# Layer 0 attention: the gates are read in place as strided columns instead of being copied for each unit

## The chip, the cores and the metric

The kernel runs on one core of a Trainium2 chip. The metric is the device time of one execution in microseconds (us); several executions are given with their median. TensorE does matrix products, VectorE and ScalarE work elementwise on SBUF and PSUM, GpSimd works elementwise on SBUF alone, and SyncE issues the DMAs. In the profile TensorE is PE (its weight loads are PEld), VectorE is DVE, ScalarE is ACT, GpSimd is POOL and SyncE is SP.

## The reference

A decoder of two layers on 1024 tokens of width 1024. Layer 0 mixes by attention with three branches, each over the same query head, and adds the three results weighted by a sigmoid gate that depends on the token, the head and the branch:

```python
gates = jax.nn.sigmoid(gate_logit + gate_b).reshape(B, S, N_MIX_HEADS, 3)
...
p_cmp = masked_softmax(s, cmp_end[None, :] <= t[:, None])      # 63 compressed blocks
o_cmp = einsum(p_cmp, vc)
o_slc = einsum(masked_softmax(s, m_sel), vg)                   # causal, 1024 keys
o_win = einsum(masked_softmax(s, m_win), vw)                   # window of 512 keys
return g[..., 0:1] * o_cmp + g[..., 1:2] * o_slc + g[..., 2:3] * o_win
```

There are 12 heads in 2 groups; 4 more heads attend to 256 memory tokens without a gate. No compressed block is visible to the first 31 tokens, so `o_cmp` is zero in those rows: the kernel reaches this by setting the compressed branch's gate to zero there (the row mask `self.rv`, one where the token's row is at least 31 and zero before). A convolutional feed-forward part follows each layer's attention; layer 1 has attention without gates.

## The kernel before, in words

Tokens lie on the 128 partitions in 8 tiles. `layer0_proj` (L706) projects them; the gate logits of tile t go to `self.gates[:, t, :]` (a tile of 128 x 8 x 36 numbers, 36 being 12 heads by 3 branches, branch last), by L755, and one sigmoid on ScalarE over all of it (L756) ends that. `self.gates` stays in SBUF.

`layer0_attn` then runs 24 gated units, one for each head h and each half c of the tokens (512 queries, four tiles of 128), and 8 memory units between them. The generator `units0` describes a unit: the selected branch (tile `ps`), the window branch (`pw`) and the compressed branch (`pc`), the last scored jointly with the window. The function `attention` (L446) is one loop of steps that interleaves a unit's stages, several units deep: a unit's `load` and its scores (PE, L300) begin about 9 steps ahead of its own value steps. In a step, DVE and ACT and POOL do:

- `lift` (L330, DVE): score plus mask from PSUM into `ps`, `pw` or `pc`, and the row minimum of the negated scores into `stat`.
- L343 and L346 (ACT): the exponentials, with their sums.
- L354 and L355 (DVE): 1 / max(sum, 1e-30) in `stat`, on 128 x 4 or 128 x 8 numbers.
- L366 (POOL): the probabilities times that reciprocal times the gate, a tile of 128 queries at a time, each with two numbers per partition as scalars (`r[:, ii:ii+1]` and `gate[:, ii:ii+1]`); for the compressed branch L360 (POOL) multiplies the four reciprocals by the four gates, and L362 (POOL) applies them to `pc`.
- L399 (PE): transposes the probabilities into PSUM (`psb`); L406 (ACT) and L409 (DVE) split them into a high and a low part in `pt`; L422 (PE) multiplies them by the values.

Besides, POOL adds the halves of finished outputs (L481, `wr`) and does one step of the rotary embedding (L623, `rt`).

`load` in `units0` also makes the unit's own copy of the gates: a tile `gt` (128 x 3 x 4, two buffers) is filled by a copy on DVE (L836), and for the first half (c = 0) the row mask is multiplied into one column (L838, DVE). Since `gt` has two buffers, the copy of one unit overwrites the `gt` of the unit two before it, and the last reader of that is the unit's L360 on POOL. The framework's scheduler sets the order of instructions on each engine and puts semaphore waits where tiles are reused; each engine runs its instructions in that order.

Of the kernel before, what the change touches and what calls it, by code (L numbers as in the profile page):

```python
# [8 lines left out]
F32 = mybir.dt.float32  # L9
# [3 lines left out]
ALU = mybir.AluOpType  # L13
# [4 lines left out]
P = 128  # L18
# [20 lines left out]
def f32(ap):  # L39
    return ap.bitcast(F32)  # L40


class Trunk:
# [674 lines left out]
    def layer0_proj(self, cpool):  # L718
        nc, a, tc = self.nc, self.a, self.tc
        w = a["a_w_in"][0]  # L720
        self.mem = []
        self.qd0 = self.dp.tile([2, 2, NH * 32, S], F32, name="qd0")
        self.kd0 = self.dp.tile([2, 2, 4 * 32, S], F32, name="kd0")
        self.vd0 = self.dp.tile([S, 4, 2 * HD], F32, name="vd0")
        self.qm0 = self.dp.tile([2, NMH * HD, S], F32, name="qm0")
        self.gates = self.cp.tile([P, NT, NH * 3], F32, name="gates")
        self.kc = self.cp.tile([P, NG, 64], F32R, name="kc")
        self.vc = self.cp.tile([P, NG, 2, HD], F32R, name="vc")
        with tc.tile_pool(name="l0p", bufs=1) as pool:
            h = [self.hpair() for _ in range(2)]  # L730
            xs = []

            def load_x(t):
                xs.append(self.sb(pool, [P, D], F32, "xl", 2))
                nc.sync.dma_start(xs[t], a["x"][0, t * P:(t + 1) * P, :])

            def norm(t):
                self.norm_t(pool, xs[t], gb, h[t // 4][0], h[t // 4][1], (t % 4) * P)
            load_x(0)
            gb = self.gain(pool, a["attn_norm"][0:1, :], 2)  # L740
            wv = self.load_block(w, [(1152, 128), (1408, 164)])
            gbias = pool.tile([P, NH * 3], F32, name="gbias")
            nc.sync.dma_start(gbias, a["a_gate_b"].to_broadcast([P, NH * 3]))
            norm(0)
            for t in range(NT):
                if t + 1 < NT:
                    load_x(t + 1)
                    norm(t + 1)
                ps = self.psb()[:, 0:292]
                hh, hl = h[t // 4]  # L750
                o = (t % 4) * P
                for kt in range(KT):
                    self.mm3(ps, (hh[:, kt, o:o + P], hl[:, kt, o:o + P]), wv(kt, 0, 292), kt == 0, kt == KT - 1)
                self.store_v(pool, ps[:, 0:256], self.vd0[t * P:(t + 1) * P], 4)
                nc.vector.tensor_tensor(self.gates[:, t, :], ps[:, 256:292], gbias, ALU.add)  # L755
            nc.scalar.activation(self.gates, self.gates, AF.Sigmoid)  # L756
            self.masks(pool, cpool)
            ct = pool.tile([P, 2, 32], F32, name="ct")
            nc.sync.dma_start(ct, a["rope_cmp"])
            comp = [self.compress(pool, h, w, kind, ct) for kind in range(2)]  # L760
            mems = [self.mem_kv(pool, l) for l in range(2)]
            keys = self.rope_proj(cpool, h, w, [(1024, 128), (1280, 128)], self.kd0, 0, None)
            first = self.rope_proj(cpool, h, w, [(0, 256)], self.qd0, 0, QSC)
            order = "k cc kkk m kkk dd kkkk m kkk c kkk m d q m c q m c q m d q m d q n c q n d q n c q n d qq n qq n q n qqqqqq"
            gens = {"k": keys, "q": first, "c": comp[0], "d": comp[1], "m": mems[0], "n": mems[1]}
            for name in order.replace(" ", ""):
                next(gens[name], None)
            for g in (comp[0], comp[1], mems[0], mems[1], first):
                for _ in g:
                    pass  # L770
        return h
# [23 lines left out]
    def units0(self, ap):  # L795
        nc = self.nc
        t_s, t_w, t_c = [("ps0", 1280, 1), ("ps1", 3328, 1)], [("pw0", 1280, 1), ("pw1", 2560, 1)], ("pc", 256, 2)
        for g in range(NG):
            kk, vv = {}, {}
            vc = self.vc[:, g].rearrange("n s d -> n (s d)")  # L800
            for h in range(g * 6, g * 6 + 6):
                for c in range(2):
                    sp_c = {ii: (0, 64, self.m_cmp[:, c * 4 + ii, :]) for ii in range(4)}
                    sp_w = {}
                    for ii in range(4):
                        i = c * 4 + ii
                        k0 = max(0, i - 4) * P
                        sp_w[ii] = (k0, (i + 1) * P, self.m_win if i >= 4 else self.m_cau[:, S - (i + 1) * P:])
                    brs = [{"spans": self.causal(c, self.m_cau), "kb": P, "p": t_s[c], "on": "pool"},
                           {"spans": sp_w, "kb": P, "p": t_w[c], "on": "pool"},  # L810
                           {"spans": sp_c, "kb": 64, "p": t_c, "on": "pool"}]

                    brs[1]["joint"] = brs[2]

                    def load(g=g, h=h, c=c, kk=kk, vv=vv, vc=vc, brs=brs):
                        if not kk:
                            for b in range(2):

                                kk[b] = self.sb(ap, [P, NT, 192] if b else [P, NT, P], F32R, f"kk{b}", 1)
                                for i in range(2):  # L820
                                    for half in range(2):
                                        p0, r0 = i * HD + half * 32, (b * NG + g) * 32
                                        nc.sync.dma_start(f32(kk[b][p0:p0 + 32, :, 0:P]), self.kd0[i, half, r0:r0 + 32, :].rearrange("r (t n) -> r t n", n=P))
                                if b:
                                    nc.vector.tensor_copy(kk[b][:, :, P:], f32(self.kc[:, g, :]).rearrange("p (o n) -> p o n", o=1).to_broadcast([P, NT, 64]))
                                vt = self.sb(ap, [P, NT, P], F32R, "vv", 2)
                                nc.sync.dma_start(f32(vt), self.vd0[:, b * NG + g, :].rearrange("(t p) d -> p t d", p=P))
                                vv[b] = vt
                        q = [self.sb(ap, [P, CH], F32R, f"qq{i}", self.n_q if i else 2) for i in range(2)]
                        for i in range(2):  # L830
                            for half in range(2):
                                for x in range(2):
                                    p0 = (i ^ x) * HD + half * 32
                                    nc.sync.dma_start(f32(q[x][p0:p0 + 32, :]), self.qd0[i, half, h * 32:(h + 1) * 32, c * CH:(c + 1) * CH])
                        gt = self.sb(ap, [P, 3, 4], F32, "gt", 2)
                        nc.vector.tensor_copy(gt, self.gates[:, c * 4:(c + 1) * 4, h * 3:(h + 1) * 3].rearrange("p t b -> p b t"))  # L836
                        if c == 0:
                            nc.vector.tensor_tensor(gt[:, 0, 0:1], gt[:, 0, 0:1], self.rv, ALU.mult)  # L838
                        for b in range(2):
                            k = kk[b] if b else kk[b].rearrange("p t n -> p (t n)")  # L840
                            brs[b].update(q=q, k=(k, k), v=lambda j, v=vv[b]: v[:, j, :], gate=gt[:, 1 + b, :])
                        brs[2].update(v=lambda j: vc, gate=gt[:, 0, :])
                    yield {"branches": brs, "load": load, "needs": [("q", h // 4)] if h >= 4 else [], "at": (h, c)}


# [722 lines left out]
```

## Time and profile before

| what | value |
|---|---|
| median of 3 runs | 2611.74 us |
| the runs | 2602.53, 2613.72, 2611.74 us |
| profiled execution, first to last instruction (span) | 2602.7 us |
| profiled execution, time of its own around the span | none listed apart from the runs |
| PE, DVE, ACT, POOL busy over the span | 95%, 73%, 52%, 29% |
| layer 0 attention in the trace | about 165 to 645 us |
| POOL instructions on gates: L366, L360 | 192, 24 |
| DVE instructions on `gt`: L836, L838 | 24, 12 |

In rows of the timeline the columns are start in us, duration in us, engine, line, operation, what is written and read, count, and in brackets the engine's idle time just before and what ended it. Rows of waits give the waiting engine and what it waited for, then the total in us, the number of waits, the longest. Rows of groups give the busy time and the mean duration in ns, then the idle time ahead of the group.

### The profile page before, as it was taken

The page shows a single profiled execution, that of the slowest core. Times are in us where ns is not written, and L with a number is a line of the kernel's source. Part 1 is how long each engine was busy: PE and PEld are TensorE (multiplying, and loading weights), DVE is VectorE, ACT ScalarE, POOL GpSimd, SP SyncE. Part 2 cuts the span into 40 slices and gives each one's busy share as a digit, 9 for nine tenths or more (in the row PEclk, how much of TensorE's full clock was granted, in tenths as well). Part 3 has the DMA queues.
Part 4 walks back from the last instruction along what each step waited for, and adds up shares of the span by engine and source line. Part 5 has one row for each costly group of instructions (what it writes and reads, how often), then busy time and mean ns, then how long its engine had stood idle before and what let it go on. Part 6 is the DMA issues. An engine that isn't in the chain of part 4 may idle for free.

```text
span 2602.7 us, 35727 instructions
## 1 busy us (share of the span) xinstructions
PE 2466.1 (95%) x12306; PEld 2058.2 (79%) x12306; DVE 1887.8 (73%) x3207; ACT 1342.2 (52%) x2553; POOL 751.8 (29%) x616
## 2 busy tenths in 40 slices
PE   7898988988999999998999999999999999998998
PEld 7787777766778888886888988887777888886886
DVE  5757787888377878877665467878476778787765
ACT  5437777877145454443454356767244444443443
POOL 0105344444134554543000000000233455444000
PEclk9999999999999999999999999999999999999999
DMA  8473224333422333347334466666622233237523
GB/s 250 145 206 111 62 82 114 104 105 125 163 74 89 113 101 98 105 169 268 108 128 137 153 186 189 199 180 176 211 101 76 95 105 114 98 100 278 172 97 114
DMA packets 302701, 357.69 MB, mean 137 GB/s; under 512 B 37960, under 2 KB 183224, under 8 KB 302520
## 3 DMA queue, kind: packets, MB, share of 16 engines
q1 hardware_dynamic: 302520, 355.41, 42.9%
q8 instruction: 97, 1.59, 0.3%
q14 instruction: 84, 0.69, 0.1%
HBM read 245.55 MB, written 109.78 MB: 137 GB/s over the span
## 4 chain that ended last, share of the span: by engine, by line
PE 71%; DVE 10%; ACT 6%; DMA 5%; POOL 4%; issue 3%; SPq 0%; POOLq 0%; ACTq 0%; DVEq 0%
PE psa L157 12%; PE psa L158 12%; PE psa L159 12%; PE psb L157 9%; PE psb L159 9%; PE psb L158 8%; PE psa L300 3%; PE psb L399 3%; PE psb L422 3%; DVE pt L409 2%; ACT pt L406 1%; POOL gs L1360 1%; DVE ps L330 1%; POOL pw L366 1%; DVE wl L82 1%
## 5 line engine op out<-in xcount | busy, mean ns | idle before, releaser
L81 ACT ACTIVATE wh<-wr 128x512 fp32r<-128x512 f32 (+2 forms) x254 | 193.0, 763 | 357.6 <-PE psb L159 146.2
L82 DVE TENSOR_TENSOR wl<-wr,wh 128x512 fp32r<-128x512 f32 (+2 forms) x254 | 241.1, 953 | 166.8 <-ACT wh L81 166.1
L1345 DVE SCALAR_TENSOR_TENSOR v<-u,cw,v 128x1023 f32<-128x1023 f32 (+1 forms) x176 | 283.1, 1608 | 68.7 <-ACT v L1343 68.5
L409 DVE TENSOR_TENSOR pt<-psb,pt 128x512 fp32r<-128x512 f32 (+2 forms) x380 | 246.6, 658 | 62.1 <-ACT pt L406 59.0
L1343 ACT ACTIVATE v<-u,cw 128x1024 f32<-128x1024 f32 x88 | 109.6, 1246 | 309.9 <-DVE u L1332 283.2
L406 ACT ACTIVATE pt<-psb 128x512 fp32r<-128x512 f32 (+2 forms) x380 | 213.4, 571 | 88.7 <-PE psb L399 83.5
L422 PE MATMUL psb<-pt,vv 128*128 128x512 f32 (+2 forms) x864 | 225.8, 356 | 17.3 <-DVE pt L409 13.2
L157 PE MATMUL psa<-hT,wh 128*128 128x512 f32 x560 | 219.2, 392 | 5.3 <-DVE u L1306 5.3
L159 PE MATMUL psa<-hT,wl 128*128 128x512 f32 x560 | 218.7, 391 | 0.8 <-DVE wl L82 0.8
L158 PE MATMUL psa<-hT,wh 128*128 128x512 f32 x560 | 218.6, 390 | 0.0
L300 PE MATMUL psa<-kk,qq 128*128 128x512 f32 (+4 forms) x792 | 186.1, 350 | 20.1 <-DVE stat L330 12.3
L343 ACT ACTIVATE ps<-ps,stat 128x128 f32<-128x128 f32 (+1 forms) x192 | 147.8, 771 | 56.8 <-DVE stat L330 56.3
L422 PEld LDWEIGHTS psb<-pt,vv 128*128 128x128 f32 x864 | 141.4, 191 | 42.2 <-DVE pt L409 21.7
L121 POOL TENSOR_TENSOR rs<-ss,consts 128x1 f32<-128x1 f32 x44 | 25.8, 588 | 511.2 <-DVE ss L119 372.5
L481 POOL TENSOR_TENSOR wr<-wr 128x512 f32<-128x512 f32 x32 | 41.4, 1300 | 427.4 <-DMA kd<-st 244.5
L399 PE MATMUL psb<-consts,ps 128*128 128x128 f32 x928 | 149.2, 279 | 14.5 <-DVE pt L409 7.5
L157 PE MATMUL psb<-wh 128*128 128x512 f32 x352 | 139.8, 397 | 20.7 <-ACT wh L81 20.6
L157 PE MATMUL psb<-hT,wh 128*128 128x512 f32 x384 | 156.6, 408 | 1.0 <-DVE pt L409 0.9
L1247 POOL TENSOR_TENSOR ws<-wr 128x512 f32<-128x512 f32 x44 | 67.7, 1539 | 295.3 <-DMA wr<-in_w_up_dram 276.2
L159 PE MATMUL psb<-hT,wl 128*128 128x512 f32 x384 | 151.2, 394 | 0.0
L158 PE MATMUL psb<-hT,wh 128*128 128x512 f32 x384 | 150.8, 393 | 0.0
L300 PEld LDWEIGHTS psa<-kk,qq 128*128 128x128 f32 x792 | 121.6, 194 | 36.1 <-DVE stat L330 13.8
(287 smaller groups left out, 6831.0 us busy)
## 6 DMA issues: line engine op xcount, KB each, us to landing
wr<-in_w_up_dram SPq DMA_DIRECT2D x88, 512.0 KB
wr<-gd SPq DMA_DIRECT2D x154, 256.0 KB
gd<-v SPq DMA_DIRECT2D x88, 256.0 KB
gd<-gs SPq DMA_DIRECT2D x66, 256.0 KB
o<-ob SPq DMA_DIRECT2D x128, 128.0 KB
wr<-o SPq DMA_DIRECT2D x32, 512.0 KB
hT<-in_w_down_dram SPq DMA_DIRECT2D x64, 256.0 KB
qd<-st SPq DMA_DIRECT2D x56, 256.0 KB
```

The costliest lines, as they stand in the source:

```text
L81: nc.scalar.activation(hi, src, AF.Copy)
L82: nc.vector.tensor_tensor(lo, src, f32(hi), ALU.subtract)
L157: mm(out, lh, rh, start=first, stop=False, skip_group_check=more)
L158: mm(out, lh, rl, start=False, stop=False, skip_group_check=more)
L159: mm(out, ll, rh, start=False, stop=last, skip_group_check=more)
L300: nc.tensor.matmul(out, w, rhs, start=b not in banks[:i], stop=b not in banks[i + 1:])
L343: nc.scalar.activation(p, p, AF.Exp, bias=st[:, 0, ii:ii + 1], scale=-1.0, accum_out=st[:, 1, ii:ii + 1])
L399: nc.tensor.transpose(tp[0:kb, x:x + P], br["pt"][ii][:, o:o + kb], self.ident)
L406: nc.scalar.activation(st["hi"], st["src"], AF.Copy)
L409: self.nc.vector.tensor_tensor(st["lo"], st["src"], f32(st["hi"]), ALU.subtract)
L422: self.nc.tensor.matmul(out, v, t, start=st["begin"] and i == 0, stop=st["end"] and i == len(mms) - 1)
L1345: nc.vector.scalar_tensor_tensor(v[:, d:], u[:, :S - d], cw[:, tap, i:i + 1], v[:, d:], ALU.mult, ALU.add)
```

## The change

After the sigmoid one instruction on DVE multiplies the row mask into the compressed branch's gate of all 12 heads in the first token tile, in place (12 numbers in a partition, 3 apart). The tile `gt` and its copy and mask for each unit go; a unit's gates are now slices of `self.gates` of four numbers in a partition, 36 numbers (144 bytes) apart.

```diff
             nc.scalar.activation(self.gates, self.gates, AF.Sigmoid)
+            g0 = self.gates.rearrange("p t (h b) -> p t h b", b=3)[:, 0, :, 0]
+            nc.vector.tensor_scalar(g0, g0, self.rv, None, ALU.mult)
...
-                        gt = self.sb(ap, [P, 3, 4], F32, "gt", 2)
-                        nc.vector.tensor_copy(gt, self.gates[:, c * 4:(c + 1) * 4, h * 3:(h + 1) * 3].rearrange("p t b -> p b t"))
-                        if c == 0:
-                            nc.vector.tensor_tensor(gt[:, 0, 0:1], gt[:, 0, 0:1], self.rv, ALU.mult)
+                        gt = [self.gates[:, c * 4:(c + 1) * 4, h * 3 + b] for b in range(3)]
                         for b in range(2):
                             k = kk[b] if b else kk[b].rearrange("p t n -> p (t n)")
-                            brs[b].update(q=q, k=(k, k), v=lambda j, v=vv[b]: v[:, j, :], gate=gt[:, 1 + b, :])
-                        brs[2].update(v=lambda j: vc, gate=gt[:, 0, :])
+                            brs[b].update(q=q, k=(k, k), v=lambda j, v=vv[b]: v[:, j, :], gate=gt[1 + b])
+                        brs[2].update(v=lambda j: vc, gate=gt[0])
```

The lines behind it move: L836 and L838 are gone, and the new instruction is L758 of the changed kernel. Lines up to L756, all of `attention` and its helpers among them, keep their numbers.

On DVE, where the scores of one unit are lifted and the copy for the next unit stands among them (the names are tiles with the program's numbers, what waits is in brackets), the kernel before has:

```order
L330 ISA ps_417_2563,stat_2562<-psa_2553,caub 128x128 [waits PE_49]
L330 ISA stat_2562 128x1
L330 ISA ps_417_2563,stat_2562<-psa_2553,caub 128x256
L330 ISA stat_2562 128x1
L330 ISA ps_417_2563,stat_2562<-psa_2553,caub 128x384
L330 ISA stat_2562 128x1
L836 COPY gt_2736<-gates 128x12 [waits Pool_49]
L409 TENSOR_TENSOR pt_2572<-psb_2567,pt_2572 64x512 [waits Activation_49]
L330 ISA ps_417_2563,stat_2562<-psa_2590,caub 128x512 [waits PE_49]
```

The changed kernel has in the same place:

```order
L330 ISA ps_412_2551,stat_2550<-psa_2541,caub 128x128 [waits PE_49,Pool_49]
L330 ISA stat_2550 128x1
L330 ISA ps_412_2551,stat_2550<-psa_2541,caub 128x256
L330 ISA stat_2550 128x1
L330 ISA ps_412_2551,stat_2550<-psa_2541,caub 128x384
L330 ISA stat_2550 128x1
L409 TENSOR_TENSOR pt_2560<-psb_2555,pt_2560 64x512 [waits Activation_49]
L330 ISA ps_412_2551,stat_2550<-psa_2578,caub 128x512 [waits PE_49]
```

The copy and its wait on POOL are gone, nothing else in this place has moved, and the first L330 (each is followed by a row that reads out its accumulator) of the unit now names POOL among its own waits.

On DVE again, some 12 us later in the trace, before the next unit's first scores are lifted, the kernel before has:

```order
L355 RECIPROCAL stat_2562<-stat_2562 128x8 [waits DVE_49]
L409 TENSOR_TENSOR pt_2695<-psb_2690,pt_2695 128x512 [waits Activation_49]
L836 COPY gt_2949<-gates 128x12 [waits Pool_49]
L409 TENSOR_TENSOR pt_2713<-psb_2708,pt_2713 128x512 [waits Activation_49]
L838 TENSOR_TENSOR gt_2949<-gt_2949,consts 128x1 [waits DVE_49]
L409 TENSOR_TENSOR pt_2723<-psb_2718,pt_2723 128x512 [waits Activation_49]
L330 ISA ps_450_2758,stat_2757<-psa_2738,caub 128x640 [waits PE_49]
```

And the changed kernel:

```order
L355 RECIPROCAL stat_2550<-stat_2550 128x8 [waits DVE_49]
L409 TENSOR_TENSOR pt_2683<-psb_2678,pt_2683 128x512 [waits Activation_49]
L409 TENSOR_TENSOR pt_2701<-psb_2696,pt_2701 128x512 [waits Activation_49]
L409 TENSOR_TENSOR pt_2711<-psb_2706,pt_2711 128x512 [waits Activation_49]
L330 ISA ps_444_2744,stat_2743<-psa_2724,caub 128x640 [waits PE_49,Pool_49]
```

Both instructions on `gt` have left the row between the splits; the rest stands as it stood. Over the whole program DVE has 36 instructions fewer and one more, POOL has the same ones in the same order (with `gates` in the place of `gt`), and on PE, ACT and SP a few single rows change places with near neighbours.

## The prediction

> **What bounds the kernel now.** I read the page first, then the busy time by stretches, then who waited for whom inside layer 0's attention, then the timeline at each copy of the gates.
>
> ```profile
> span 2602.7 us, 35727 instructions
> 165.00:645.00 480.00, 427.42 (x2586) 356.84 (x2586) 380.49 (x1059) 347.47 (x857) 217.76 (x273) 0.99 0.37 108
> ```
>
> The second row is the stretch with the 24 gated units: 480.00 us, then busy time of PE, PEld, DVE, ACT, POOL. PE works for 427.42 of 480 us, so about 52.6 us of idle PE is all that a better order there can win. DVE comes next with 380.49 us; POOL works for less than half of it. The change touches nothing outside this stretch but one instruction. So the question is which of PE's 52.6 us go back to the instructions that are removed. The waits of this stretch, PE's and DVE's:
>
> ```profile
> PE psa L300 <- DVE stat L330: 12.1, 11, 2.6
> PE psb L422 <- DVE pt L409: 9.4, 11, 1.9
> PE psb L399 <- DVE pt L409: 8.6, 10, 2.2
> DVE gt L836 <- POOL stat L360: 16.0, 11, 2.3
> ```
>
> The first three rows show that PE, when it waits, mostly waits for DVE: 30.1 us for the scores (L330, which frees the score banks) and for the split (L409). The fourth shows DVE itself standing still for 16.0 us in 11 of the 24 copies, until POOL has read the gates of the unit two before. DVE takes its instructions in order, so what stands queued behind a waiting copy is just those L409 and L330.
>
> ```profile
> L836 DVE COPY gt<-gates 128x12 f32<-128x12 f32 x24 | 4.0, 169 | 16.0 <-POOL stat L360 16.0
> L838 DVE TENSOR_TENSOR gt<-gt,consts 128x1 f32<-128x1 f32 x12 | 5.6, 471 | 0.2
> ```
>
> **What goes.** 24 copies with 4.0 us, 12 masks with 5.6 us and the 16.0 us of waiting: 25.6 us of DVE time. The mean of the masks, 471 ns for one number in a partition, is itself odd; one of them stands below, 1.21 us long, and it ends as POOL's instruction ends (271.48 + 1.21 = 272.69; 271.41 + 1.26 = 272.67).
>
> 25.6 us is the most that the removal itself can give, and zero the least: it pays only where PE stands idle behind it. So I go through the places. The plainest wait, from the timeline:
>
> ```profile
> 255.08 3.45 POOL L366 TENSOR_SCALAR pw<-pw,stat,gt 128x640 f32<-128x640 f32 x4 [5.58 <-DVE stat L355]
> 256.14 0.58 ACT L406 ACTIVATE pt<-psb 64x512 fp32r<-64x512 f32 x1
> 258.73 0.17 DVE L836 COPY gt<-gates 128x12 f32<-128x12 f32 x1 [2.26 <-POOL stat L360]
> 258.93 0.69 DVE L409 TENSOR_TENSOR pt<-psb,pt 64x512 fp32r<-64x512 f32 x1
> 259.67 0.66 PE L399 MATMUL psb<-consts,ps 128*128 128x128 f32 x4 [2.25 <-DVE pt L409]
> ```
>
> POOL needs 3.45 us for four normalisations; DVE arrives early, idles 2.26 us, copies, and only then does the split L409 whose input ACT had ready at 256.72. PE, which needs the bank that L409 frees, idles for 2.25 us. Without the copy L409 would start at 256.72, 2.2 us earlier. The stall passes to PE in full. The same pairs elsewhere:
>
> ```profile
> 270.79 0.17 DVE L836 COPY gt<-gates 128x12 f32<-128x12 f32 x1 [1.97 <-POOL stat L360]
> 271.41 1.26 POOL L481 TENSOR_TENSOR wr<-wr 128x512 f32<-128x512 f32 x1
> 271.48 1.21 DVE L838 TENSOR_TENSOR gt<-gt,consts 128x1 f32<-128x1 f32 x1
> 274.08 1.09 PE L300 MATMUL psa<-kk,qq 128*128 128x512 f32 x4 [2.13 <-DVE stat L330]
> ...
> 306.22 0.17 DVE L836 COPY gt<-gates 128x12 f32<-128x12 f32 x1 [1.04 <-POOL stat L360]
> 306.43 0.47 DVE L838 TENSOR_TENSOR gt<-gt,consts 128x1 f32<-128x1 f32 x1
> 308.29 1.10 PE L300 MATMUL psa<-kk,qq 128*128 128x512 f32 x4 [1.76 <-DVE stat L330]
> ...
> 364.17 0.17 DVE L836 COPY gt<-gates 128x12 f32<-128x12 f32 x1 [1.42 <-POOL stat L360]
> 365.09 0.63 PE L399 MATMUL psb<-consts,ps 128*128 128x128 f32 x4 [1.00 <-DVE stat L354]
> ...
> 374.16 0.17 DVE L836 COPY gt<-gates 128x12 f32<-128x12 f32 x1 [1.97 <-POOL stat L360]
> 376.39 1.09 PE L300 MATMUL psa<-kk,qq 128*128 128x512 f32 x4 [1.08 <-DVE stat L330]
> ...
> 438.64 0.17 DVE L836 COPY gt<-gates 128x12 f32<-128x12 f32 x1 [2.17 <-POOL stat L360]
> 439.58 1.02 PE L399 MATMUL psb<-consts,ps 128*128 128x128 f32 x4 [1.95 <-DVE pt L409]
> ```
>
> For each place I take the smaller of DVE's lost time and PE's idle time behind it: 2.25; 2.13 (of 3.35); 1.68 (1.04 + 0.17 + 0.47, PE idles 1.76); 1.00; 1.08; 1.95. These six give 10.1 us. Three more are doubtful:
>
> ```profile
> 227.13 0.17 DVE L836 COPY gt<-gates 128x12 f32<-128x12 f32 x1 [1.40 <-POOL stat L360]
> 232.32 0.66 PE L399 MATMUL psb<-consts,ps 128*128 128x128 f32 x4 [1.96 <-ACT ob L513]
> ...
> 342.07 1.26 DVE L838 TENSOR_TENSOR gt<-gt,consts 128x1 f32<-128x1 f32 x1
> 347.02 0.50 PE L422 MATMUL psb<-pt,vv 128*128 128x512 f32 x1 [1.34 <-DVE pt L409]
> ...
> 595.58 0.17 DVE L836 COPY gt<-gates 128x12 f32<-128x12 f32 x1 [1.05 <-POOL stat L360]
> 595.67 1.75 DVE L354 TENSOR_SCALAR stat<-stat 128x4 f32<-128x4 f32 x1
> 598.27 0.51 PE L422 MATMUL psb<-pt,vv 128*128 128x512 f32 x1 [1.92 <-DVE pt L409]
> ```
>
> At 227 PE waits for ACT, five us later; at 342 other work of DVE and POOL lies between; at 595 an L354 of 1.75 us follows, which the change leaves there. Their smaller sides are 1.57, 1.26 and 1.22, 4.05 us together, bounded below by zero; halfway is 2.0 us. At the remaining waits and copies PE did not idle behind DVE, or by a few tenths; I count nothing.
>
> **What comes.** The mask on the gates of all heads is one DVE instruction of 12 numbers in a partition, behind the sigmoid. There DVE is idle:
>
> ```profile
> 58.96 1.23 DVE L82 TENSOR_TENSOR wl<-wr,wh 128x1024 fp32r<-128x1024 f32 x1 [4.64 <-ACT wh L81]
> ```
>
> It has 4.64 us of cover and should last as a copy of 12 numbers does, about 0.17 us; nothing is queued behind it but this L82, which waits for ACT. Without that cover it would cost its 0.17 us, once.
>
> The first L330 of a unit's `ps`, `pw` and `pc` now carries a wait on POOL of its own (39 rows in all). Those waits were missing only because the copy ahead had already waited for a later POOL instruction; the `ps` that L330 overwrites was read by POOL before PE transposed it. I price them at nothing; if each condition took as long as a whole copy, 0.17 us, that would be 6.6 us of DVE, and if it hands POOL's state on to engines that waited for it themselves, a little less than nothing.
>
> POOL's own rows on the gates:
>
> ```profile
> L366 POOL TENSOR_SCALAR ps<-ps,stat,gt x96: 447/873/1802, 199.9 to 622.9; 128x128 f32<-128x128 f32 x12, 128x256 f32<-128x256 f32 x12, 128x384 f32<-128x384 f32 x12, 128x512 f32<-128x512 f32 x12
> L360 POOL TENSOR_TENSOR stat<-stat,gt x24: 191/201/218, 207.3 to 635.7; 128x4 f32<-128x4 f32 x24
> PEld psb L399 <- POOL ps L366: 3.8, 4, 1.3
> ```
>
> L366 takes one gate per partition, which has no stride to feel; only L360 reads four numbers 144 bytes apart. Its 201 ns for four numbers are mostly a fixed cost. I take zero, and price the other end below.
>
> **The sum.** 10.1 + 2.0 = 12.1 us off the profiled 2602.7 us, so 2590.6 us for an execution like that one. The profile gives no time of that execution around its span, and its span lies at the low end of the runs (2602.53 to 2613.72); I take the same 12.1 us off the median: 2611.7 - 12.1 = 2599.6 us, 0.46% less. Half a percent, 13.1 us, is about what a measurement of this kernel can tell from no change; the forecast stops just short of it.
>
> [...] The mask that ends with POOL's instruction was one row. The other is the longest L354:
>
> ```profile
> 576.97 3.46 DVE L354 TENSOR_SCALAR stat<-stat 128x4 f32<-128x4 f32 x1
> ```
>
> L354 does on four numbers what the copy does on twelve in 0.17 us, so some DVE instructions on SBUF wait inside themselves while POOL works. [...]
>
> **The rivals.**
>
> 1. DVE's time is the bound itself, so all of it counts: PE waits for DVE at 30.1 us worth of places, more than I tied to the copies. Then 25.6 us go: 2586.1 us. Against it: at 10 or so copies PE did not idle. Chance 0.21 for anything from 16 us up.
>
> 2. The stall comes back under another name: DVE gets to its next L354 sooner, and that meets POOL's run of L366, which the copy's wait used to sit out. A meeting at a random moment of the 3.45 us run costs half, 1.7 us; six of them 10.4 us, which leaves 1.7 us of the gain: 2610.0 us. For it: 576.97. Against it: in the order around 258.73 the copy stands ahead of its unit's last L330, and L354 needs ACT's sums behind that L330, so that POOL has most of its run behind it by then. Chance 0.24, for gains of 1 to 8 us.
>
> 3. The change doesn't do what it says: the waits that now stand on the L330 rows hold DVE as long as the copies did. Then of the sum only what the instructions themselves took stays, 0.17 us at eight of the nine places and masks of 1.21, 0.47 and 1.26 us, 4.3 us: 2607.4 us. Against it: the data they wait for is older. Chance 0.04.
>
> 4. Slower. POOL pays for every strided gate: each L366 and L360 takes another 0.2 us, the price of a whole L360. A unit has 8 L366 and one L360, so its probabilities come 1.8 us later; PE already waits for POOL at four places (3.8 us). If each of 24 units passed that on, 43.2 us would come on top: 2642.8 us. It is slower by over half a percent once 25.2 of the 43.2 us reach PE, that is 14 of the 24 units. Against it: POOL idles for 5.58 us ahead of the quoted run, and L366 reads one number. [...] Chance 0.05.
>
> **How the numbers follow.** The forecast, a gain of 8 to 16 us, has 0.46. Just under half of it lies beyond 13.1 us, which with rival 1 makes faster 0.21 + 0.21 = 0.42; the other 0.25 with rivals 2 and 3 makes same 0.53; rival 4 is slower, 0.05. The range goes from 2587, nearly all of rival 1, to 2611, nearly all of rivals 2 and 3; outside lie rival 4 and a run of measurements as far apart as the ones before (11 us).
>
> **What would show it.** Right: no DVE row waits for L360; the PE idle of 2.25, 2.13 and 1.95 us at those three places is gone; PE's idle time in the stretch falls from 52.6 to about 40 us, the stretch from 480 to about 468 us, with L360 still near 0.2 us and L366 near its old medians. Wrong: L354 rows over 1 us at more places than before (rival 2), L330 waiting for POOL (3), longer L366 (4), or a stretch shorter by more than 16 us (1).

## The result, and the profile after

| | before | changed |
|---|---|---|
| median of 4 runs each, us | 2611.26 | 2592.20 |
| the runs, us | 2602.53 to 2613.72 | 2587.84 to 2595.78 |
| ratio, 95% interval | | 0.9928 [0.9907, 0.9950] |
| the profiled execution: span, us | 2602.7 | 2592.9 |

The changed kernel is faster by 18.8 us by the ratio (0.0072 x 2611.26), more than the half percent that can be told from no change. The forecast, 12.1 us, had the sign and the mechanism and was too small. The measured 2592.2 us lies within the range of 2587 to 2611 us, but not where I had put the largest chance: 0.53 for a time within half a percent of before. One of the 57 executions of the kernel before that were timed beside the experiments below took 3475.8 us, at a granted clock of 0.654, and is left out of the ratios and of the line by clock below.

The page of the changed kernel, and its busy time in the stretch of layer 0's attention (the columns are the stretch, PE, PEld, DVE, ACT, POOL, the granted clock, the DMA share and GB/s):

```profile
span 2592.9 us, 35691 instructions
165.00:635.00 470.00, 430.78 (x2625) 360.40 (x2624) 374.37 (x1025) 348.16 (x860) 218.37 (x273) 0.99 0.39 112
```

There are 36 instructions fewer. Of the stretch now shown, 10 us shorter than the one of before, PE works through a little more (430.78 against 427.42 us) and is idle for 470.00 - 430.78 = 39.2 us, where it was 52.6: 13.4 us less. Between the same two PE instructions (those at 165.04 and 645.00 us before) the traces give 479.97 us before, 461.84 us changed, 18.1 us less, and 465.49 us, 14.5 us less, when the change was run again. The idle time of PE in it falls by 13.4 and 13.3 us; PE is busy for 4.7 us and 1.1 us less. So the fall of the idle time comes again, and the other part mostly does not. A stretch shorter by more than 16 us was the prediction's sign of its rival 1, and the first pair of traces shows it; the experiments, not this number, decide about that rival.

The waits in the stretch now shown, PE's and then DVE's:

```profile
PE psb L422 <- DVE pt L409: 9.9, 15, 1.3
PE psa L300 <- DVE stat L330: 6.9, 10, 2.6
PE psb L399 <- DVE pt L409: 3.8, 6, 0.8
```

```profile
DVE pt L409 <- ACT pt L406: 33.8, 66, 1.6
...
DVE rt L622 <- POOL rt L623: 5.3, 3, 2.4
```

PE's three largest waits for DVE, 30.1 us before, are 20.6 us. DVE's 16.0 us for L360 have no successor: the one row left in which DVE waits for POOL is the rotary embedding's (5.3 us; 3.9 us before), and no L330 waits for POOL although 39 more of them name it than before. More of DVE's waits are for ACT instead (66 of them for L406, 52 before), so DVE now stands idle more often for ACT, and PE waits for DVE for less time.

The place at which the prediction saw the plainest stall, from the timeline of the changed kernel (start, duration, engine, line; in brackets the idle time ahead and what ended it):

```profile
255.12 3.45 POOL L366 TENSOR_SCALAR pw<-pw,stat,gates 128x640 f32<-128x640 f32 x4 [5.55 <-DVE stat L355]
...
256.72 0.68 DVE L409 TENSOR_TENSOR pt<-psb,pt 64x512 fp32r<-64x512 f32 x1 [0.22 <-ACT pt L406]
...
257.46 0.66 PE L399 MATMUL psb<-consts,ps 128*128 128x128 f32 x4
...
258.54 0.20 POOL L360 TENSOR_TENSOR stat<-stat,gates 128x4 f32<-128x4 f32 x1
258.82 0.61 POOL L362 TENSOR_TENSOR pc<-pc,stat 128x256 f32<-128x256 f32 x1
...
259.02 0.43 DVE L354 TENSOR_SCALAR stat<-stat 128x4 f32<-128x4 f32 x1
```

POOL does the same run at the same time as before. L409 starts at 256.72, as soon as ACT's half is ready, and not at 258.93; L399 starts at 257.46 with no idle PE ahead of it, where it started at 259.67 after 2.25 us. The last row is a small meeting with POOL: 0.43 us for an instruction whose median is 0.17, and it ends as L362 does (259.02 + 0.43 = 259.45; 258.82 + 0.61 = 259.43).

To see where the time comes from along the whole attention, I took the start of the n-th PE instruction in both traces and the difference of the two. It falls in steps at the places of before (worked out from the two traces, us):

| place (us of before) | forecast | changed | the change run again |
|---|---|---|---|
| 259.67 | 2.25 | 2.31 | 2.29 |
| 274.08 (seen at 271.6) | 2.13 | 2.28 | 2.31 |
| 308.29 | 1.68 | 1.61 | 1.61 |
| 365.09 | 1.00 | 0.99 | 0.97 |
| 376.39 (375.0) | 1.08 | 1.28 | 1.26 |
| 439.58 | 1.95 | 2.52 | 2.53 |
| the six | 10.1 | 11.0 | 11.0 |
| the doubtful: 232, 347 | 2.0 with the next | 0.95, 0 | |
| the doubtful: 598.27 | | 1.94 | 1.94 |
| 580.71 | none | 3.12 | 3.17 |

At 439.58 the first PE instruction comes 2.11 us sooner; the rest of the 2.52 us is PE running at half its clock in the kernel before (0.50, last section), so the six without it give 10.6 us. Some steps of half a microsecond (331, 416, 450) and the clock's episodes, below, come on top; the changed kernel enters the attention 0.9 us behind, and at the last L422 of layer 0 it is 17.2 us ahead.

The place at 580.71 was not among mine. Before, by the timeline (the L354 of 3.46 us stands between these rows and was quoted above):

```profile
576.10 1.29 POOL L481 TENSOR_TENSOR wr<-wr 128x512 f32<-128x512 f32 x1
...
577.34 0.62 POOL L362 TENSOR_TENSOR pc<-pc,stat 128x256 f32<-128x256 f32 x1
...
577.91 2.49 POOL L481 TENSOR_TENSOR wr<-wr 128x512 f32<-128x512 f32 x2
...
580.71 0.56 PE L300 MATMUL psa<-kk,qq 128*128 128x512 f32 x2 [2.84 <-DVE stat L355]
```

And the same L354 in the changed kernel:

```profile
563.20 1.28 POOL L481 TENSOR_TENSOR wr<-wr 128x512 f32<-128x512 f32 x1
...
564.07 0.45 DVE L354 TENSOR_SCALAR stat<-stat 128x4 f32<-128x4 f32 x1
...
564.45 0.61 POOL L362 TENSOR_TENSOR pc<-pc,stat 128x256 f32<-128x256 f32 x1
...
565.02 2.53 POOL L481 TENSOR_TENSOR wr<-wr 128x512 f32<-128x512 f32 x2
```

Before, L354 began in the first of four POOL instructions (576.97) and ended with the last (577.91 + 2.49 = 580.40; 576.97 + 3.46 = 580.43). In the changed kernel it begins 0.87 us into the same first instruction and ends with that one (563.20 + 1.28 = 564.48; 564.07 + 0.45 = 564.52), and PE's 2.84 us behind it are gone.

### The profile page after: what moved, and what is told of

The parts are those of the page before. It is cut to its first block, busy times and chain, and to the rows that moved or that the text cites. A ratio compares the mean times of both kernels' runs of the same rounds, so it can differ in the third digit from the quotient of the medians.

```text
span 2592.9 us, 35691 instructions
## 1 busy us (share of the span) xinstructions
PE 2467.9 (95%) x12306; PEld 2058.8 (79%) x12306; DVE 1869.4 (72%) x3172; ACT 1341.3 (52%) x2553; POOL 757.6 (29%) x616
## 4 chain that ended last, share of the span: by engine, by line
PE 74%; DVE 8%; ACT 6%; DMA 5%; POOL 3%; issue 3%; SPq 0%; POOLq 0%; ACTq 0%; DVEq 0%
PE psa L157 12%; PE psa L158 12%; PE psa L159 12%; PE psb L157 9%; PE psb L159 9%; PE psb L158 9%; PE psb L399 4%; PE psb L422 4%; PE psa L300 4%; DVE pt L409 2%; ACT pt L406 1%; POOL gs L1359 1%; DVE wl L82 1%; DMA hT<-in_w_down_dram 1%; DVE ps L330 1%
## 5 line engine op out<-in xcount | busy, mean ns | idle before, releaser
L82 DVE TENSOR_TENSOR wl<-wr,wh 128x512 fp32r<-128x512 f32 (+2 forms) x254 | 242.5, 959 | 166.2 <-ACT wh L81 165.5
L1344 DVE SCALAR_TENSOR_TENSOR v<-u,cw,v 128x1023 f32<-128x1023 f32 (+1 forms) x176 | 275.4, 1565 | 68.8 <-ACT v L1342 67.2
L409 DVE TENSOR_TENSOR pt<-psb,pt 128x512 fp32r<-128x512 f32 (+2 forms) x380 | 247.1, 660 | 66.7 <-ACT pt L406 63.9
L406 ACT ACTIVATE pt<-psb 128x512 fp32r<-128x512 f32 (+2 forms) x380 | 213.4, 572 | 88.0 <-PE psb L399 82.0
L422 PE MATMUL psb<-pt,vv 128*128 128x512 f32 (+2 forms) x864 | 225.9, 356 | 18.2 <-DVE pt L409 12.2
L300 PE MATMUL psa<-kk,qq 128*128 128x512 f32 (+4 forms) x792 | 185.1, 348 | 13.3 <-DVE stat L330 7.0
L121 POOL TENSOR_TENSOR rs<-ss,consts 128x1 f32<-128x1 f32 x44 | 25.8, 589 | 514.0 <-DVE ss L119 375.0
L422 PEld LDWEIGHTS psb<-pt,vv 128*128 128x128 f32 x864 | 141.2, 191 | 43.5 <-DVE pt L409 21.0
L1246 POOL TENSOR_TENSOR ws<-wr 128x512 f32<-128x512 f32 x44 | 76.5, 1739 | 296.4 <-DMA wr<-in_w_up_dram 256.6
L399 PE MATMUL psb<-consts,ps 128*128 128x128 f32 x928 | 148.4, 277 | 8.1 <-DVE pt L409 3.4
L330 DVE CUSTOM_DVE_ANT_0 ps<-psa,caub 128x128 f32<-128x128 f32 (+1 forms) x192 | 139.0, 751 | 14.9 <-PE psa L300 14.7
```

The source lines that it names most:

```text
L82: nc.vector.tensor_tensor(lo, src, f32(hi), ALU.subtract)
L300: nc.tensor.matmul(out, w, rhs, start=b not in banks[:i], stop=b not in banks[i + 1:])
L330: self.nc.vector.tensor_tensor_reduce(p, s, br["spans"][ii][2], -1.0, 3e38, ALU.add, ALU.min, br["stat"][:, 0, ii:ii + 1])
L399: nc.tensor.transpose(tp[0:kb, x:x + P], br["pt"][ii][:, o:o + kb], self.ident)
L406: nc.scalar.activation(st["hi"], st["src"], AF.Copy)
L409: self.nc.vector.tensor_tensor(st["lo"], st["src"], f32(st["hi"]), ALU.subtract)
```

## The experiments

The theory: DVE stands still at a copy until POOL has read the old gates, and that standing still is the gain; the copies and masks as work are worth nothing. The rivals: the DVE time of the copies and masks counts itself; the locks between DVE and POOL decide, so the gain depends on how L354 falls; the strided read costs POOL something that hides part of the gain. By a lock I mean no more than what rows of the kernel before show, a DVE instruction on few numbers that lasts until an instruction of POOL ends: L838 took 1.21 us at 271.48 (median 0.16), and L354 1.75 us at 595.67 (median 0.17), to 597.42, where an L362 of POOL ends at 595.50 + 1.89 = 597.39. All kernels were timed in 5 rounds beside the kernel before on the same chip, in three groups, each on another chip (the medians of the kernel before: 2608.78 us beside the four kernels with other buffers or masks, 2611.28 us beside the strided read and the kernel before without L354, 2608.61 us beside the rest).

### More buffers for the copies

The first try takes the copies' wait away by giving `gt` four buffers in the kernel before:

```diff
-                        gt = self.sb(ap, [P, 3, 4], F32, "gt", 2)
+                        gt = self.sb(ap, [P, 3, 4], F32, "gt", 4)
```

> The kernel before with four buffers for the copied gates instead of two: copies and masks stay on VectorE, but a copy overwrites what was read four units before, so it should not have to wait for GpSimd. Theory (the waits of VectorE for GpSimd's L360 are the gain): the 16.0 us of idle before L836 goes to under 1 us, PE's gaps of 2.25, 2.13 and 1.95 us at the quoted places go, and the time falls by 11 to 16 us, most of the change's own gain of about 19 us. Rival (VectorE's instruction time is the gain, 9.6 us of copies and masks): within 3 us of before, since every instruction is still there.

Measured: 2607.17 us, ratio 0.9997 [0.9986, 1.0008]: nothing. But the wait was not taken away. DVE's waits, the group of the copies (durations min/median/max in ns, first and last start), and the place near 259 us:

```profile
DVE gt L836 <- POOL stat L360: 15.1, 10, 2.3
```

```profile
L836 DVE COPY gt<-gates x24: 142/170/178, 169.3 to 556.6; 128x12 f32<-128x12 f32 x24
```

```profile
259.66 0.17 DVE L836 COPY gt<-gates 128x12 f32<-128x12 f32 x1 [2.28 <-POOL stat L360]
```

The last copy starts at 556.6 us, and at 595.58 before: with more buffers each copy is put further ahead in DVE's order, up to where its buffer comes free, and there it meets the L360 of an older unit just the same (15.1 us in 10 waits). So this run says nothing against the theory, which missed in its expectation: buffers are no cure where a copy is issued as early as its buffer allows.

### The masks, and the copies without the masks

The row mask is applied once behind the sigmoid, L838 goes, the copies stay with their two buffers:

```diff
             nc.scalar.activation(self.gates, self.gates, AF.Sigmoid)
+            g0 = self.gates.rearrange("p t (h b) -> p t h b", b=3)[:, 0, :, 0]
+            nc.vector.tensor_scalar(g0, g0, self.rv, None, ALU.mult)
...
-                        if c == 0:
-                            nc.vector.tensor_tensor(gt[:, 0, 0:1], gt[:, 0, 0:1], self.rv, ALU.mult)
```

> The kernel before with the row mask applied once to all heads (as in the change), while each unit still copies its gates into two buffers: the waits and copies stay, the 12 masks (5.6 us of VectorE, 3.9 us of it beyond their shortest) go. Theory: the idle before the copies stays near 16 us and the time falls by 0 to 4 us. Rival (the masks, locked behind GpSimd's instructions, are the gain): falls by more than 8 us.

Measured: 2610.02 us, 1.0003 [0.9992, 1.0014]. The 5.6 us that 12 masks took on DVE are worth nothing that shows (the interval leaves room for 2.1 us). The copies' wait stands:

```profile
DVE gt L838 <- POOL stat L360: 16.1, 11, 2.3
```

(L838 is the copy in this kernel.) The same with four buffers:

```diff
-                        gt = self.sb(ap, [P, 3, 4], F32, "gt", 2)
+                        gt = self.sb(ap, [P, 3, 4], F32, "gt", 4)
```

> Both of the above together: mask once, four buffers, so that of the old work only the 24 copies (4.0 us of VectorE) stay. Theory: within 4 us of the changed kernel, a fall of 14 to 19 us. Rival (the instructions count): falls by less than 10 us.

Measured: 2607.49 us, 0.9996 [0.9986, 1.0006], with 14.8 us of wait in 10. Like the first, and a miss of the expectation too: the wait is still there, and so is the time.

### More wait

```diff
-                        gt = self.sb(ap, [P, 3, 4], F32, "gt", 2)
+                        gt = self.sb(ap, [P, 3, 4], F32, "gt", 1)
```

> The kernel before with one buffer for the copied gates: a copy now has to wait for GpSimd's reads of the unit just before it, so the suspected wait is made longer and nothing else is added. Theory: idle before L836 well over 16 us and the time longer than before by 10 us or more. Rival (the wait is hidden and only instruction time counts): within 3 us of before.

Measured: 2629.06 us, 1.0075 [1.0059, 1.0091]. DVE's waits:

```profile
DVE gt L836 <- POOL stat L360: 29.4, 20, 2.3
```

Same instructions, 13.4 us more of waiting in 9 more places, 20 us more of time (16 us at the same granted clock, by the line in the next section). The time follows the wait.

### The same copies with and without their wait

This pair settles it. Both are the changed kernel with one DVE copy for each unit put back, of the four gates that L360 reads. In one, each copy has a place of its own in a tile for all 24 units, so that nothing has to come free:

```diff
+        gall = ap.tile([P, 24, 4], F32, name="gt")
...
+                        gc = gall[:, h * 2 + c]
+                        nc.vector.tensor_copy(gc, gt[0])
+                        gt[0] = gc
```

> The changed kernel with a copy put back on VectorE for each unit: the four gates of the compressed branch, which L360 reads, are copied into a place of the unit's own (24 places, none reused), so 24 copies are done and none waits for GpSimd. Theory (the wait is the gain): as fast as the changed kernel within 3 us, some 16 to 19 us under before. Rival (the copies are what costs, since four buffers gained nothing): within 5 us of before.

In the other, the copies share two buffers:

```diff
+                        gc = self.sb(ap, [P, 4], F32, "gt", 2)
+                        nc.vector.tensor_copy(gc, gt[0])
+                        gt[0] = gc
```

> The same 24 copies of four gates, but into two buffers in turn, so that each waits for GpSimd's L360 of two units before; masks stay applied once. Theory: about 16 us of idle before the copies is back and with it the time of before, within 4 us, that is 15 to 19 us slower than the same copies without the wait. Rival (the wait is hidden): as fast as the one without the wait, within 3 us.

Measured: 2592.84 us, 0.9933 [0.9918, 0.9948], without the wait; 2613.01 us, 1.0012 [1.0002, 1.0022], with it. 24 copies of the same numbers on the same engine: 20.2 us between them, 15.8 at the same granted clock (the line in the next section), and each comes out near one of the two kernels, the one with the wait 3 us above the kernel before. The group of the copies and the place near 259 us in the kernel without the wait:

```profile
L840 DVE COPY gt<-gates x24: 157/163/1257, 170.2 to 177.2; 128x4 f32<-128x4 f32 x24
```

```profile
258.42 0.69 DVE L409 TENSOR_TENSOR pt<-psb,pt 64x512 fp32r<-64x512 f32 x1 [0.22 <-ACT pt L406]
...
259.17 0.66 PE L399 MATMUL psb<-consts,ps 128*128 128x128 f32 x4
```

With nothing to wait for, all 24 copies are done by 177.4 us, ahead of the first unit, and L409 follows ACT. In the kernel with the wait:

```profile
DVE gt L839 <- POOL stat L360: 16.1, 11, 2.3
```

```profile
258.59 0.20 POOL L360 TENSOR_TENSOR stat<-stat,gt 128x4 f32<-128x4 f32 x1
...
258.82 0.17 DVE L839 COPY gt<-gates 128x4 f32<-128x4 f32 x1 [2.26 <-POOL stat L360]
259.02 0.68 DVE L409 TENSOR_TENSOR pt<-psb,pt 64x512 fp32r<-64x512 f32 x1
...
259.76 1.12 PE L399 MATMUL psb<-consts,ps 128*128 128x128 f32 x4 [2.25 <-DVE pt L409]
```

DVE idles 2.26 us until L360 has ended, the copy goes, then L409, and PE's 2.25 us are back, to the hundredth. One thing differs between the two besides the wait, and follows from it: where the copies stand in DVE's order.

The change once more beside them:

> The changed kernel itself, timed beside the others on this chip. Theory: 16 to 20 us under before, as measured. Rival (part of the 19 us was the drift between two sets of runs): 10 to 14 us under, as forecast.

Measured: 2594.34 us, 0.9938 [0.9924, 0.9952], 16.2 us by the ratio; with the same steps as the first time (third column above).

### The strided read

The changed kernel with the gates stored so that a unit's four stand 4 bytes apart:

```diff
-        self.gates = self.cp.tile([P, NT, NH * 3], F32, name="gates")
+        self.gates = self.cp.tile([P, NH * 3, NT], F32, name="gates")
...
-                        gt = [self.gates[:, c * 4:(c + 1) * 4, h * 3 + b] for b in range(3)]
+                        gt = [self.gates[:, h * 3 + b, c * 4:(c + 1) * 4] for b in range(3)]
```

> The changed kernel with the gates laid out the other way round, head and branch outside and token tile inside, so that GpSimd reads a unit's four gates 4 bytes apart instead of 144. Theory (the stride costs nothing): within 3 us of the changed kernel, L360 at 0.20 us. Rival (strided reads cost GpSimd up to 0.2 us an instruction): L360 shorter by 20 ns or more and the time 3 us or more under the changed kernel.

Measured: 2594.38 us, 0.9933 [0.9918, 0.9947], so as the change. The group of L360 in the changed kernel, and in this one:

```profile
L360 POOL TENSOR_TENSOR stat<-stat,gates x24: 194/204/214, 208.2 to 618.6; 128x4 f32<-128x4 f32 x24
```

```profile
L360 POOL TENSOR_TENSOR stat<-stat,gates x24: 196/206/222, 207.4 to 622.4; 128x4 f32<-128x4 f32 x24
```

204 ns with the stride, 206 without, 201 from the copy before: the stride costs nothing that shows. That the 201 ns are mostly a fixed cost, as the prediction has it, is an estimate that the kernel before bears out: its L366 on `ps` take 448 ns on 128 x 128 and 1200 ns on 128 x 1024 (means), 0.84 ns for each number more, at which four numbers come to about 3 ns.

### The locks

L354 keeps the sum from being zero (the maximum of the sum and 1e-30); the rows with 3.46, 1.75 and 0.43 us are its. Here it is left out of the changed kernel, and the reciprocal reads the sum itself:

```diff
-        nc.vector.tensor_scalar(st[:, 2], st[:, 1], 1e-30, None, ALU.max)
-        nc.vector.reciprocal(st[:, 2], st[:, 2])
+        nc.vector.reciprocal(st[:, 2], st[:, 1])
```

> The changed kernel without L354: the sum is at least one for every row, since its largest term is exp(0), so the maximum with 1e-30 changes nothing, and L355 takes the reciprocal straight from the sums. That takes away the VectorE instruction that waits inside itself while GpSimd works (12.6 us in 56 instructions of layer 0's attention, the longest 1.2 us). Theory (the lock still costs): 3 to 10 us under the changed kernel. Rival (the lock lies where TensorE has work): within 3 us of it.

Measured: 2587.49 us, 0.9915 [0.9899, 0.9930]: 22.2 us by the ratio, 6 us more than the change in the same group, and the fastest kernel of the study. Leaving L354 out takes away more than its locks: its own 0.17 us in each place go too, and so does a step between ACT's sums and POOL's normalisation. This run does not separate them.

The same edit in the kernel before:

> The kernel before, copies, masks and waits in place, without L354 (the maximum of the sums with 1e-30, which changes nothing since each sum is at least one). Theory (the lock of L354 behind GpSimd's instructions is a cost of its own, 7.0 us beyond 56 times 175 ns in this kernel, beside that of the copies' waits): 3 to 8 us under before, as much as its removal gave in the changed kernel. Rival (the two overlap: what L354 loses the copies' wait would lose anyway): within 3 us of before.

Measured: 2599.17 us, 0.9951 [0.9936, 0.9967], 12.8 us by the ratio, about twice what it gives in the changed kernel and more than was expected. DVE's waits:

```profile
DVE gt L835 <- POOL stat L359: 12.6, 11, 2.2
```

(one line higher here, the copy and the multiplication are the same.) The copies' wait has fallen too, from 16.0 to 12.6 us, perhaps because DVE and POOL now meet at other moments. The two gains overlap: 16.2 and 12.8 us apart, 22.2 us together. Part of that is the clock, as the next section works out.

## Why the prediction was right, and where its size was off

**The wait was the gain: shown.** Copies without a wait cost nothing that shows (2592.84 us) and copies with it cost the whole change (2613.01 us). That DVE's order would let L409 and L330 go ahead, and that PE stood behind them, held at each of the six places: 11.0 us, 10.6 without the half clock at 439.58, against 10.1 us.

**The masks and copies as work: nothing that shows.** Rival 1 had the DVE time count in full. It is out as a mechanism: masks taken away 1.0003, copies put back without a wait 0.9933 against 0.9938 for the change beside it. By size alone the first comparison, 18.8 us, the 16.2 us of the second and the 18.1 us of the stretch all lie where I had put that rival: size did not tell the two apart, the copies with and without the wait did.

**The doubtful places: 2.9 us where I had taken half of 4.05.** At 598 all came back and more (1.94 us for a bound of 1.22): the L354 next to that copy took 1.75 us, and 0.17 us at the same place in the changed kernel (580.05). At 347 nothing came back, at 232 0.95 us.

**The term that failed: "At the remaining waits and copies PE did not idle behind DVE, or by a few tenths; I count nothing."** It left out what a shifted DVE does to its other meetings with POOL. I had looked at L354 only as a loss (rival 2: it meets POOL's run at the six places). The meetings came, but short. The group of the 32 of four numbers, before and in the changed kernel (busy time, mean ns, then the idle time ahead):

```profile
L354 DVE TENSOR_SCALAR stat<-stat 128x4 f32<-128x4 f32 x32 | 11.8, 368 | 9.1 <-ACT ps L343 5.2 <-ACT pm L340 3.8
```

```profile
L354 DVE TENSOR_SCALAR stat<-stat 128x4 f32<-128x4 f32 x32 | 8.1, 252 | 10.8 <-ACT ps L343 5.7 <-ACT pm L340 5.0
```

They became shorter by 3.7 us, not longer: three L354 of layer 0's attention take over 1 us before and one in the changed kernel, so the sign set for rival 2 did not come. The worst of them, 3.46 us, gave PE back 3.1 us at 580.71. That gift is luck of the moments and no property of reading in place: it came again when the change was run again, but the kernel with copies and no wait still has the long row, and so has the one with the gates 4 bytes apart (3.49 us at 564.66), which has no copy at all. The last two are as fast as the changed kernel within what can be told; and two kernels whose copies wait, the one with four buffers and the one with the masks applied once, have no L354 over 1.75 us and are no faster than before. So the step at 580.71 stands in the traces but the times do not show it. The long row of the kernel with copies and no wait:

```profile
566.36 3.47 DVE L354 TENSOR_SCALAR stat<-stat 128x4 f32<-128x4 f32 x1
```

That a long L354 can cost PE time is shown at 580.71, where PE's 2.84 us of idle time goes with it. Taking L354 out (22.2 us against 16.2 us in one group) fits that, but takes its work away as well; how much of the change's own gain is the locks' I know only from the steps in the traces.

**Rivals 3 and 4.** No L330 waits for POOL, so 3 is out. 204 and 206 ns, and the same time with and without the stride, put 4 out. The cover for the new mask was there; the timeline of the changed kernel:

```profile
55.44 0.24 DVE L758 TENSOR_SCALAR gates<-gates,consts 128x12 f32<-128x12 f32 x1 [0.51 <-ACT gates L756]
...
59.62 1.22 DVE L82 TENSOR_TENSOR wl<-wr,wh 128x1024 fp32r<-128x1024 f32 x1 [3.95 <-ACT wh L81]
```

0.24 us (0.17 were forecast), then still 3.95 us of idle DVE ahead of L82.

**How large is it?** Each execution is listed with its mean granted clock, and the time goes with it: in a straight line through the 56 executions of the kernel before that are listed with a clock beside the experiments and the 9 of the changed kernel, 1.7 us for each 0.001. The mean clocks are 0.9857 and 0.9871. At the clock that both have most often, 0.986, the medians are 2608.9 us (24 executions) and 2594.7 us (5): 14.2 us, and the line gives 14.3 us (the executions scatter by 2.5 us about it, so it is good to about 2 us). So the change is worth about 14 us at the same clock, close to the 13.4 us by which PE's idle time fell; of the 4.5 us by which the 18.8 us of the first comparison exceed that, the mean clocks make 2.5 us (0.00145 at 1.7 us for each 0.001), and the rest is within the scatter of four executions against four. Of the 6.7 us between 18.8 us and the forecast of 12.1 us, then, 2.2 us belong to the places and 4.5 us to the clock and the scatter, for which the prediction had no term. The change run again comes to 13.7 us on the line, inside the 10 to 14 us that its rival named. The clock also tells why the spans of the two profiled executions lie only 9.8 us apart: the one of before had 0.988, the one of the changed kernel 0.986, and behind the attention, from 650 us to the end of the span, the clock was at 0.50 for 43 us before and for 60 us in the changed kernel. On the same line the two runs without L354 come to 8.2 us (before) and 17.3 us (changed), against 14.3 for the change alone, so at the same clock leaving out L354 is worth 8.2 us before and 3.0 us after; 3.4 of the 8.2 us are as much as the copies' wait lost there. The rest of the overlap is argued, not shown.

**Is the higher clock the change's own doing?** Nine executions don't tell, but all kernels together do in part. The four in which no copy waits (the changed one, the same again, copies without a wait, gates 4 bytes apart) have a mean clock of 0.9867 in 20 executions; the five in which 10 or 11 copies wait (the kernel before, more buffers, masks once, both, copies with the wait) have 0.9854 in 104. The difference, 0.0013, is more than three times its standard error (0.0004), and the order is the same in each group that has both kinds. The clock goes with the idle time of PE in the stretch measured between the same two instructions: 0.9838 with 64.8 us (one buffer), 0.9857 with 52.6 us (before), 0.9872 with 44.6 us (before without L354), 0.9871 with 39.2 us (changed), 0.9884 with 38.5 us (changed without L354); the six others lie between, 0.9849 to 0.9866 with 53.6 to 40.7 us, the idle time being that of one trace each. So part of the higher clock is likely the change's own, and 14 us is its gain with that part taken out. That fewer gaps raise the clock is not shown by a run made for it.

## What to carry to other kernels

A tiny copy into a reused buffer can hold a whole in-order queue, as DVE stood here for 16.0 us at 11 of 24 copies: look not at what the copy takes (4.0 us for 24) but at who last read the buffer, how late that engine is, and what is queued behind the copy. Price such a wait place by place, by the smaller of the waiting engine's loss and the bottleneck's idle time behind it; that gave 10.1 us of a measured 10.6 here at the six places, and the steps elsewhere lay in meetings that shift when the engine comes earlier. More buffers don't help where a copy is issued as soon as its buffer is free (15.1 us of wait and 2607.17 us with four); reading in place (2592.20 us), or a slot for each user so that the copies can all be made ahead (2592.84 us), does.

## What the runs showed of the hardware

A small DVE instruction that met a run of POOL instructions was held through several of them in one trace and through one in another: L354 on 128 x 4 took 3.46 us, from the first of four to the end of the last, in the kernel before, and 0.45 us, to the end of the first, at the same place in the changed kernel; its median is 0.17 us in both. No run here explains why it ended with the fourth instruction in the one and with the first in the other.

The granted clock falls to 0.50 for short stretches in these traces. Three neighbouring stretches of the kernel before, in the columns of the busy-time view (the granted clock is the number after POOL's):

```profile
436.00:440.00 4.00, 2.05 (x15) 1.76 (x14) 1.76 (x5) 2.28 (x8) 3.21 (x5) 0.97 0.05 13
440.00:443.00 3.00, 3.00 (x15) 2.82 (x14) 2.17 (x9) 1.30 (x3) 1.28 (x3) 0.50 0.00 0
443.00:447.00 4.00, 4.00 (x25) 3.45 (x24) 2.82 (x17) 3.79 (x13) 1.10 (x2) 0.98 0.40 99
```

It is 0.50 for three microseconds just behind the PE idle of 1.95 us that ends at 439.58, and close to full again after. The changed kernel has no such stretch there, and once the clock is back, at 444 us, it is 3.15 us further ahead than before that place, where 1.95 us were idle. That the idle time brought the low clock on is what these rows suggest; it was not tried, and idle time alone does not decide it: behind the same 2.25 us of PE idle near 259 us the clock from 260 to 263 us was 1.00 in the kernel before and 0.50 in the kernel with copies and the wait.
